# Block products summed in place in PSUM, and merge gates set between the recurrences

## The chip, the cores and the metric

The kernel runs on one core of one Trainium2 chip. The metric is the device time of one execution in microseconds (us). Before the change three runs gave 2738.37, 2735.38 and 2736.16 us, median 2736.16 us.

A core has five engines that matter here, each with its own instruction queue, worked off in order: TensorE (PE: matmuls, and PEld: the loading of their stationary operand), VectorE (DVE), ScalarE (ACT), GpSimd (POOL), and SyncE (SP, which here issues the DMAs). They wait for each other through semaphores. Matmul results land in PSUM, which has 8 banks of 128 partitions x 512 float32; PE writes it, DVE and ACT read it.

## The reference, cut to what matters

One layer of a hybrid mixer over 2048 tokens of width 1024, in float32:

```
h = rmsnorm(x, norm_g);  u = h @ w_in            # one wide input projection
A: RG-LRU   (lru_x, lru_z): conv of 4 taps, two block-diagonal gates, a linear scan, times silu(lru_z)
B: mLSTM    (m_x, m_o, m_z): conv of 4 taps, silu, chunkwise matrix memory
C: HGRN2    (h_q, h_f, h_i, h_z);  D: GLA (g_q, g_k, g_v, g_lr, g_z): gated linear attention in chunks
merged = sum over the 4 branches of sigmoid(merge_n) * (y_n @ w_branch[n])
out = rmsnorm(x + merged @ w_out, final_g)
```

The projection makes, among others, 32 channel tiles (128 channels each) of merge gates and 4 + 4 tiles for the RG-LRU.

## The kernel before

The tokens go in two halves of 1024 (called A and B here; A runs from about 52 us on, B from about 1422 us on). For each half there is a stretch of *pairs* (`ahead_pairs`), then the mixers B, C and D (`mixers`), then the branch projections and gates (`merge`) and the output projection (`outp`). In A and B alike the pairs take some 700 us, a quarter of the time each.

**A pair** (`ip_pair`) is the projection of two tiles of 128 channels for 1024 tokens. It is a 2 x 2 block product (channels tile 0 or 1, tokens 0 to 511 or 512 to 1023, contraction halves of 512 channels) in Winograd's form: seven block products in place of eight. The products are named by their left operand, a block of the input or a sum of blocks: `a11`, `a12`, `a22`, `s1`, `s2`, `s3`, `s4`. The input blocks and their sums are made once per half (`split_blocks`, lines L306 and L375 to L378). The weight blocks b11, b12, b21, b22 of each pair come by DMA; their sums are made on DVE (`wsum`, L427: four per pair). Each product splits its weight block into a high and a low float32r part, high by ACT (L416, tile `wh`), low by POOL (L417, tile `wl`), six buffers of each, and then issues 12 matmuls (L422): 4 contraction tiles x (high x high, high x low, low x high).

Each of the seven products has a PSUM bank of its own, handed out round and round over all 8 banks (`bank8`; the banks' tiles are called `pb` and `mx`). The first is copied out by ACT (`c11`, L437). The outputs c11, c12, c21, c22 are tiles in SBUF (`arena`), and the sums of products are formed there by DVE: seven additions per pair, each of one SBUF tile and one bank (`add`, L431).

When a pair is done its `fin` runs: for an RG-LRU pair (`r`, four per half) silu, a convolution (L704, L706), two gates of 12 matmuls in all (L735) with their tanh, exp and sqrt (L744) on ACT, and a scan on DVE (L748); for the paths (`z`) a silu (L477) or, for the two pairs of `m_x`, a convolution with its silu on DVE and ACT (L704, L706, L763; `mconv`); for merge gates (`g`, 13 pairs per half) a tanh or nothing, and a DMA to DRAM; for `d` the decays of HGRN2. The outputs live in 10 arena units, room for two and a half pairs.

**What sets the order.** `GORD` is a list by hand of which pairs are written in which order: `r`, `z`, `g`, `d` with a count; `t` switches the activation table, `m` runs a piece of mLSTM's rows. Beyond that a list scheduler with a cost model orders each engine's queue: instructions have priorities (`prio`: EV for evacuations and weights, LAT for the RG-LRU's and the convolution's tail, which comes later), and the order it finds is fixed in the program. On the chip each engine then works its queue in that order, waiting where a semaphore isn't there yet.

Of the kernel before, what the change touches and what calls it, by code (L numbers as in the profile page):

```python
# [17 lines left out]
HT = 1024  # tokens of a half  # L18
DM = 1024
KT = 8  # k tiles of d_model  # L20
U = 516  # columns of one arena unit
NU = 16  # arena units that stay
NA = 4  # tiles of two units that are the arena's outside of the fast products
NY = 8  # the same, and branch outputs in the merge
NP = 6  # merge gates (of 32) computed between the mixers
NE = 5  # of these, so many for the first tokens while the others are split
EPS = 1e-6
NPB = 2  # PSUM banks of the input projection; the other ones are the mixers'
NG = 10  # arena units of the fast products; the other ones are what follows them
PRE = (("mx", 4), ("mo", 4), ("mz", 4), ("hq", 4), ("hz", 4), ("gz", 4), ("gq", 2), ("gk", 2))  # paths to DRAM, with their tiles  # L30
# [11 lines left out]
GORD = [('r',1),('z',2),('r',1),('z',2),('r',1),('z',2),('r',1),('z',6),('g',8),('t',0),('m',0),('g',1),('m',0),('g',1),('m',0),('g',1),('m',0),('d',0),('m',0),('g',99),('d',1),('z',2)]  # L42
NORM = {"hz": "hnw", "gz": "gnw"}  # gate paths with the norm's weight in them
SILU = ("lz", "mz", "hq", "hz", "gz")
FILL = [0, 2, 0, 0, 0, 1, 0, 0, 1, 0, 0, 0, 2, 0]  # merge gates projected before each stage of the mixers

# columns of the packed per-channel vectors
# [10 lines left out]
# channel-major column tiles of the input projection, in the order of wc  # L58
# [10 lines left out]
# constants that depend on shapes alone  # L69
# [29 lines left out]
class Arena:  # L99
    """Units of U columns, handed out in program order, round and round; pairs start at even units."""  # L100
# [47 lines left out]
class Trunk:  # L148
# [107 lines left out]
    def proj_ch(self, pieces, rh, rl, sink, ns=(0, 1)):  # L256
        """128 columns of a product for 512 tokens at a time from weight pieces of 4 k tiles
        each: sink(token slice, PSUM [128, 512])."""
# [23 lines left out]
    def ip_tok(self, pieces, ncol, evac, single=8):  # L282
        """Token-major column group: evac(first chunk, PSUM [128 tokens, chunks, ncol]); chunks one by one from some."""
# [10 lines left out]
    def ip_tok_k(self, pieces, evac, ks):  # L294
        """The same for 256 columns, k outermost: the operands' tiles are done with one by one."""
# [13 lines left out]
    def split_first(self, xs):  # L309
        """The normalised input of the first tokens"""  # L310
# [7 lines left out]
    def load_first(self, xs):  # L318
        """The first tokens, and merge gates from them before the norm's factor is known"""
# [40 lines left out]
    def split_blocks(self, xs, st):  # L360
        """The other blocks (two of tokens by two of channels) that the products take: one more as it
        is, four sums; the block left out goes to DRAM."""
# [22 lines left out]
    def restore_block(self):  # L385
        """The block left out of the products, where its sum was."""
# [13 lines left out]
    def ip_pair(self, t0, t1, fin):  # L400
        """Two column tiles of 1024 tokens each; fin of both, [128, 3 free + 1024]."""
# [9 lines left out]
        def product(x, w):  # L411
# [6 lines left out]
            ps = self.bank8()  # L418
            for k, (xh, xl) in enumerate(self.op[x]):
                ws = slice(k * 128, (k + 1) * 128)  # L420
                for i, (wp, xp) in enumerate(((hi, xh), (hi, xl), (lo, xh))):
                    nc.tensor.matmul(ps, wp[:, ws], xp, start=(k == 0 and i == 0), stop=(k == 3 and i == 2))  # L422
# [6 lines left out]
        def add(o, x, y):  # L429
            with self.prio(self.EV):  # L430
                V.tensor_tensor(o, x, y, op=ALU.add)  # L431
# [1006 lines left out]
def layout(i):  # L1438
    """The inputs laid out for the kernel: no arithmetic on the data."""
    f = {k: np.asarray(v) for k, v in i.items()}  # L1440
    z = {}
# [99 lines left out]
```

## Time and profile before

| | |
|---|---|
| median of 3 runs | 2736.16 us (2735.38 to 2738.37) |
| span of the profiled execution | 2737.5 us |
| PE busy | 2603.8 us (95%) |
| DVE, ACT, POOL busy | 1736.1, 1291.6, 1499.7 us |
| additions L431 | 462 (348 on `mx` banks and 114 on `pb` banks) |
| copies L437 | 66 |

The span of the profiled execution lies between the timed runs; no other time of it is shown. Times in the rows below are us from the span's start, durations ns where the view says so. PEclk is the share of TensorE's full clock that was granted: 1.00 is 2.4 GHz, and a stretch at 1.2 GHz counts half. "Idle before" is idle time of the engine ahead of an instruction and what ended it. A matmul's recorded duration is longer than the distance to the next one, since they overlap.

### The profile page before, as it was taken

The numbers are of one execution on the slowest core, as the hardware profiler recorded it, in microseconds if no ns is written. First come the engines' busy times: TensorE is split into PE (matmuls) and PEld (weight loads), VectorE is DVE, ScalarE is ACT, GpSimd is POOL, SyncE is SP. The second block draws the span as 40 slices with busy tenths as digits, with TensorE's granted clock in tenths as the row PEclk, the third lists the DMA queues.
The fourth block names the chain that finished last, engine by engine and source line by source line (L and its number), as shares of the span: only waits on it lengthen the run. The fifth ranks groups of instructions, "written<-read, shape, count | busy, mean of one in ns | idle before, by whom it ended". The sixth has DMA issues, their size and how long they took to land. (4 is left out here: it accounts for less than half of the span.)

```text
span 2737.5 us, 45829 instructions
## 1 busy us (share of the span) xinstructions
PE 2603.8 (95%) x16800; PEld 2153.6 (79%) x16800; DVE 1736.1 (63%) x2907; ACT 1291.6 (47%) x2763; POOL 1499.7 (55%) x1273
## 2 busy tenths in 40 slices
PE   7889999999989898999999999999999999999999
PEld 5667788877878876778977777888787888777789
DVE  8987853346667767743478878533477677776332
ACT  5554554334444565542465545533344445644433
POOL 5556644444546545567476666444455556554753
PEclk9999999999999999999999999999999999989999
DMA  6132334243454435795442322433335533458821
GB/s 227 61 109 89 101 119 139 98 145 103 148 170 128 121 121 189 253 317 165 155 138 94 110 91 89 139 116 108 135 113 179 167 118 106 146 190 308 273 93 74
DMA packets 227072, 393.03 MB, mean 144 GB/s; under 512 B 20720, under 2 KB 78080, under 8 KB 226848
## 3 DMA queue, kind: packets, MB, share of 16 engines
q1 hardware_dynamic: 226848, 390.11, 42.7%
q8 instruction: 132, 2.16, 0.3%
q14 instruction: 92, 0.75, 0.1%
HBM read 270.42 MB, written 119.60 MB: 142 GB/s over the span
## 5 line engine op out<-in xcount | busy, mean ns | idle before, releaser
L417 POOL TENSOR_TENSOR wl<-wr,wh 128x512 fp32r<-128x512 f32 x264 | 371.6, 1411 | 302.4 <-ACT wh L416 294.4
L417 POOL TENSOR_TENSOR wl<-gth,wh 128x512 fp32r<-128x512 f32 x198 | 284.4, 1437 | 294.6 <-ACT wh L416 284.2
L422 PE MATMUL mx<-s,wh 128*128 128x512 f32 x1296 | 408.5, 395 | 11.3 <-DVE s L306 4.7
L431 DVE TENSOR_TENSOR arena<-arena,mx 128x512 f32<-128x512 f32 x348 | 229.4, 681 | 221.8 <-PE mx L422 208.5
L250 POOL TENSOR_TENSOR wl<-wr,wh 128x512 fp32r<-128x512 f32 (+1 forms) x176 | 250.4, 1431 | 175.4 <-ACT wh L249 139.8
L422 PE MATMUL mx<-hh,wh 128*128 128x512 f32 x760 | 302.0, 397 | 11.9 <-DVE arena L431 10.2
L422 PE MATMUL mx<-hh,wl 128*128 128x512 f32 x760 | 302.3, 398 | 3.1 <-POOL wl L417 3.1
L422 PE MATMUL mx<-hl,wh 128*128 128x512 f32 x760 | 302.0, 397 | 2.0 <-DVE hl L306 2.0
L422 PEld LDWEIGHTS mx<-s,wh 128*128 128x128 f32 x1296 | 243.9, 188 | 70.6 <-DVE s L306 7.1
L268 PE MATMUL pb<-hh,wh 128*128 128x512 f32 x704 | 286.9, 409 | 7.4 <-ACT hh L1284 2.6
L268 PE MATMUL pb<-hl,wh 128*128 128x512 f32 x704 | 286.5, 407 | 5.8 <-DVE hl L1285 5.8
L268 PE MATMUL pb<-hh,wl 128*128 128x512 f32 x704 | 284.3, 404 | 0.0
L416 ACT ACTIVATE wh<-wr 128x512 fp32r<-128x512 f32 x264 | 164.5, 627 | 232.7 <-PE mx L422 98.4
L280 PE MATMUL pb<-wh,hh 128*128 128x256 f32 (+1 forms) x880 | 254.2, 290 | 3.7 <-ACT arena L1006 1.5
L422 PE MATMUL mx<-s,wl 128*128 128x512 f32 x648 | 256.2, 396 | 0.9 <-POOL wl L417 0.9
L280 PE MATMUL pb<-wl,hh 128*128 128x256 f32 (+1 forms) x880 | 253.4, 288 | 1.7 <-POOL wl L250 1.7
L280 PE MATMUL pb<-wh,hl 128*128 128x256 f32 (+1 forms) x880 | 253.5, 288 | 0.0
L416 ACT ACTIVATE wh<-gth 128x512 fp32r<-128x512 f32 x198 | 124.4, 629 | 246.6 <-DVE gth L427 201.6
L249 ACT ACTIVATE wh<-wr 128x512 fp32r<-128x512 f32 (+1 forms) x176 | 110.0, 629 | 161.9 <-PE pb L268 106.6
L422 PEld LDWEIGHTS mx<-hh,wh 128*128 128x128 f32 x760 | 144.3, 190 | 50.1 <-ACT arena L218 11.0
L422 PEld LDWEIGHTS mx<-hh,wl 128*128 128x128 f32 x760 | 143.6, 189 | 41.0 <-POOL wl L417 8.2
L422 PEld LDWEIGHTS mx<-hl,wh 128*128 128x128 f32 x760 | 144.0, 189 | 38.1 <-DVE hl L306 3.2
(614 smaller groups left out, 6177.6 us busy)
## 6 DMA issues: line engine op xcount, KB each, us to landing
wr<-in_wc_dram SPq DMA_DIRECT2D x246, 256.0 KB, 2.7
g<-arena SPq DMA_DIRECT2D x52, 512.0 KB, 3.4
gth<-in_wc_dram SPq DMA_DIRECT2D x66, 256.0 KB, 2.8
wr<-in_wb_dram SPq DMA_DIRECT2D x64, 256.0 KB, 3.0
hl<-y SPq DMA_DIRECT2D x32, 512.0 KB, 5.9
arena<-g SPq DMA_DIRECT2D x48, 256.0 KB, 3.9
arena<-in_xT_dram SPq DMA_DIRECT2D x32, 256.0 KB, 5.1
lw<-g SPq DMA_DIRECT2D x32, 256.0 KB, 3.4
```

Source lines behind the costliest of these rows:

```text
L249: nc.scalar.activation(hi, raw, AF.Copy)
L250: nc.gpsimd.tensor_tensor(lo, raw, hi, op=ALU.subtract)
L268: nc.tensor.matmul(ps, w[:, ws], h[:, ts], start=(k == 0 and i == 0), stop=(k == nk - 1 and i == 2))
L280: self.nc.tensor.matmul(v, h[:, cs], w[:, ws], start=(first and i == 0), stop=(last and i == 2))
L416: A.activation(hi, w, AF.Copy)
L417: G.tensor_tensor(lo, w, hi, op=ALU.subtract)
L422: nc.tensor.matmul(ps, wp[:, ws], xp, start=(k == 0 and i == 0), stop=(k == 3 and i == 2))
L431: V.tensor_tensor(o, x, y, op=ALU.add)
```

## The change

In `ip_pair` three banks (p, q, r) serve a pair instead of seven. A product with `first=True` starts a bank anew; the others are added by PE to what the bank holds, and the bank is read between two products: copied by ACT (four copies per pair, three more) or added by DVE (three additions per pair, four fewer). In `GORD` the first eight pairs of gates no longer follow the RG-LRU's and the paths' pairs in one block: two pairs come first of all, one each before the second, third and fourth RG-LRU pair, and three behind the paths. Numbers of matmuls, weight sums, splits and DMAs stay. Comments are gone from the file too.

```diff
-GORD = [('r',1),('z',2),('r',1),('z',2),('r',1),('z',2),('r',1),('z',6),('g',8),('t',0),...]
+GORD = [('g',2),('r',1),('z',2),('g',1),('r',1),('z',2),('g',1),('r',1),('z',2),('g',1),('r',1),('z',6),('g',3),('t',0),...]
...
-        def product(x, w):
+        def product(x, w, ps, first=False):
...
-            ps = self.bank8()
...
-                    nc.tensor.matmul(ps, wp[:, ws], xp, start=(k == 0 and i == 0), stop=(k == 3 and i == 2))
-            return ps
+                    nc.tensor.matmul(ps, wp[:, ws], xp, start=(first and k == 0 and i == 0), stop=(k == 3 and i == 2),
+                                     skip_group_check=not first)
...
-        def add(o, x, y):
+        def add(o, ps):
             with self.prio(self.EV):
-                V.tensor_tensor(o, x, y, op=ALU.add)
+                V.tensor_tensor(o, o, ps, op=ALU.add)
+
+        def copy(o, ps):
+            with self.prio(self.EV):
+                A.activation(o, ps, AF.Copy)
...
-        p = product("a11", b11)
-        with self.prio(self.EV):
-            A.activation(c11, p, AF.Copy)
+        p, q, r = self.bank8(), self.bank8(), self.bank8()
+        product("a11", b11, p, True)
+        copy(c11, p)
+        product("a12", b21, q, True)
+        add(c11, q)
         wsum(b11, b12, b11)
         wsum(w2, b22, b11)
-        p = product("s2", w2)
-        add(c21, c11, p)
-        p = product("s1", b11)
-        add(c12, c21, p)
+        product("s2", w2, p)
+        copy(c12, p)
+        product("s1", b11, r, True)
+        copy(c22, r)
         wsum(b12, b22, b12)
-        p = product("s4", b22)
-        q = product("s3", b12)
-        add(c22, c12, q)
-        add(c21, c21, q)
-        add(c12, c12, p)
-        p = product("a12", b21)
-        add(c11, c11, p)
+        product("s3", b12, p)
+        add(c22, p)
+        product("s4", b22, r)
+        add(c12, r)
         wsum(b21, b21, w2)
-        p = product("a22", b21)
-        add(c21, c21, p)
+        product("a22", b21, p)
+        copy(c21, p)
```

How instructions stand now, at three places. First PE in a stretch of gates of half A; `pb_98` is bank p of one pair and `mx_100` its bank r, `mx_102` is bank p of the next pair. Before, the products of a pair follow each other, each to the next bank:

```order
L422 MATMUL mx_99<-s_3_582,wl_93 128x512
L422 MATMUL mx_100<-s_4_583,wh_82 128x512 x2
...
L422 MATMUL mx_100<-s_7_586,wl_88 128x512
L422 MATMUL mx_101<-s_8_587,wh_83 128x512 x2
```

Now:

```order
L422 MATMUL pb_98<-s_3_582,wl_88 128x512
L422 MATMUL mx_100<-s_4_583,wh_83 128x512 x2
...
L422 MATMUL mx_100<-s_7_586,wl_89 128x512
L422 MATMUL mx_102<-hh_63,wh_87 128x512
...
L422 MATMUL mx_102<-hh_66,wl_93 128x512
L422 MATMUL pb_98<-hh_63,wh_84 128x512
...
L422 MATMUL pb_98<-hh_66,wl_90 128x512
L422 MATMUL mx_100<-s_8_587,wh_85 128x512 x2
```

Between `s2` (its end is the first row above) and `s3` into the same bank stand `s1` and the next pair's `a11`: two products, not one; between `s1` and `s4` into `mx_100` stand that `a11` and `s3`.

Second DVE where the convolutions of the two `m_x` pairs run in half A. L706 before and L709 now is a tap of the convolution, L763 and L766 its silu, L427 a weight sum, L431 an addition out of a bank. Before:

```order
L427 TENSOR_TENSOR gth_94<-gth_94,gth_95 128x512
L706 SCALAR_TENSOR_TENSOR arena<-arena,hmc 128x512 x6
L431 TENSOR_TENSOR arena<-arena,mx_100 128x512
L706 SCALAR_TENSOR_TENSOR arena<-arena,hmc 128x512 x2
L763 SCALAR_TENSOR_TENSOR arena<-arena 128x512
L431 TENSOR_TENSOR arena<-arena,mx_101 128x512
L763 SCALAR_TENSOR_TENSOR arena<-arena 128x512 x2
L706 SCALAR_TENSOR_TENSOR arena<-arena,hmc 128x512 x3
L431 TENSOR_TENSOR arena<-arena,mx_103 128x512 x2
```

Now:

```order
L431 TENSOR_TENSOR arena<-arena,pb_98 128x512
L709 SCALAR_TENSOR_TENSOR arena<-arena,hmc 128x512
L696 COPY carry<-arena 128x3
L709 SCALAR_TENSOR_TENSOR arena<-arena,hmc 128x512 x2
L431 TENSOR_TENSOR arena<-arena,mx_100 128x512
L695 COPY arena<-carry 128x3
L766 SCALAR_TENSOR_TENSOR arena<-arena 128x512
L709 SCALAR_TENSOR_TENSOR arena<-arena,hmc 128x512
L431 TENSOR_TENSOR arena<-arena,mx_102 128x512
L709 SCALAR_TENSOR_TENSOR arena<-arena,hmc 128x512 x3
L427 TENSOR_TENSOR wr_79<-wr_80,wr_79 128x512
```

The additions among the taps were those of the second RG-LRU pair; now they are those of the second `m_x` pair (`pb_98` and `mx_100`) and of the gate pair that stands ahead of that RG-LRU pair (`mx_102`). The row that held six taps in a run now holds three.

Third ACT behind the first RG-LRU pair: L744 before and L747 now is the sqrt of the RG-LRU, L437 and L435 a copy out of a bank, L416 and L417 the high part of a weight block, L707 the first tap of the `m_x` convolution. Before:

```order
L416 ACTIVATE wh_82<-wr_81 128x512
L744 ACT_TABLE_LOAD
L744 ACTIVATE arena<-arena 128x512
L416 ACTIVATE wh_84<-gth_94 128x512
L437 ACTIVATE arena<-mx_100 128x512
```

Now:

```order
L218 ACTIVATE arena<-arena,small 128x512
L747 ACT_TABLE_LOAD
L747 ACTIVATE arena<-arena 128x512
L417 ACTIVATE wh_87<-wr_79 128x512
L747 ACTIVATE arena<-arena 128x512
L707 ACTIVATE arena<-arena,hmc 128x512
L417 ACTIVATE wh_84<-wr_79 128x512
L435 ACTIVATE arena<-pb_97 128x512
L417 ACTIVATE wh_83<-gth_95 128x512
L435 ACTIVATE arena<-pb_98 128x512
```

The copy from `pb_97` is c22 = s1 of the first `m_x` pair; PE writes s4 to that bank only behind it. Over the program ACT has 47 table loads now, where there were 29: eight more in the pairs (two each behind the third and fourth RG-LRU pair of a half), ten more at the end of the mixers. The mixers' instructions are the same, but the scheduler has set them in another order in places.

## Rows read from the trace of the kernel before

**Rows 1.** The page: its span and PE's busy time.

```profile
span 2737.5 us, 45829 instructions
PE 2603.8 (95%) x16800; PEld 2153.6 (79%) x16800; DVE 1736.1 (63%) x2907; ACT 1291.6 (47%) x2763; POOL 1499.7 (55%) x1273
```

**Rows 2.** Windows: stretch, its length; busy (xinstructions) of PE, PEld, DVE, ACT, POOL; PEclk; DMA.

```profile
1700.00:1800.00 100.00, 100.00 (x433) 81.09 (x433) 52.39 (x77) 48.77 (x79) 50.96 (x38) 1.00 0.40 132
52.00:85.00 33.00, 23.49 (x91) 16.66 (x92) 33.00 (x49) 12.97 (x22) 22.25 (x15) 0.95 0.14 40
85.00:200.00 115.00, 101.28 (x401) 78.02 (x400) 103.63 (x132) 62.12 (x96) 66.63 (x45) 0.94 0.26 87
200.00:400.00 200.00, 199.17 (x857) 160.35 (x856) 144.09 (x178) 102.00 (x164) 122.80 (x87) 1.00 0.33 110
1422.00:1440.00 18.00, 14.55 (x60) 10.59 (x59) 13.25 (x11) 9.90 (x19) 18.00 (x13) 1.00 0.36 126
1440.00:1600.00 160.00, 146.76 (x609) 116.04 (x608) 131.71 (x165) 81.50 (x130) 92.94 (x66) 0.97 0.26 89
```

**Rows 3.** PE's waits from 85 to 200, then from 1440 to 1600: total, times, longest.

```profile
PE mx L422 <- DVE arena L431: 6.8, 2, 5.1
PE pb L422 <- POOL wl L417: 3.3, 3, 1.7
PE pb L422 <- ACT wh L416: 1.6, 1, 1.6
PE pb L735 <- POOL wl L725: 1.3, 2, 1.0
...
PE mx L422 <- DVE arena L431: 6.4, 2, 5.1
```

**Rows 4.** Windows around the longest waits of each half.

```profile
130.00:142.00 12.00, 8.74 (x25) 6.27 (x25) 12.00 (x14) 5.97 (x11) 7.49 (x5) 0.72 0.24 70
160.00:170.00 10.00, 5.53 (x17) 4.28 (x18) 9.93 (x15) 4.52 (x8) 2.23 (x3) 0.83 0.16 60
```

**Rows 5.** DVE from 84 to 178: the window, then groups by line (busy us, mean ns).

```profile
84.00:178.00 94.00, 81.06 (x313) 61.93 (x313) 88.54 (x116) 46.20 (x72) 48.66 (x33) 0.93 0.25 87
...
L706 DVE SCALAR_TENSOR_TENSOR arena<-arena,hmc 128x512 f32<-128x512 f32 x24 | 25.0, 1075 | 0.1
L431 DVE TENSOR_TENSOR arena<-arena,mx 128x512 f32<-128x512 f32 x24 | 15.8, 678 | 0.5 <-ACT arena L437 0.5
L706 DVE SCALAR_TENSOR_TENSOR arena<-arena,pvt 128x512 f32<-128x512 f32 x12 | 11.1, 959 | 0.1
L763 DVE SCALAR_TENSOR_TENSOR arena<-arena 128x512 f32<-128x512 f32 x8 | 6.4, 814 | 0.0
L427 DVE TENSOR_TENSOR wr<-wr,wr 128x512 f32<-128x512 f32 x8 | 5.7, 708 | 2.1 <-DMA wr<-in_wc_dram 2.1
L427 DVE TENSOR_TENSOR gth<-wr,wr 128x512 f32<-128x512 f32 x4 | 4.6, 1147 | 0.0
L431 DVE TENSOR_TENSOR arena<-arena,pb 128x512 f32<-128x512 f32 x6 | 4.0, 676 | 0.0
...
L306 DVE TENSOR_TENSOR s<-arena,s 128x512 fp32r<-128x512 f32 x2 | 2.5, 1235 | 0.0
L427 DVE TENSOR_TENSOR gth<-gth,gth 128x512 f32<-128x512 f32 x3 | 2.0, 679 | 0.0
```

**Rows 6.** DVE's timeline ahead of PE's longest wait, which ends at 164.47.

```profile
149.34 5.59 DVE L706 SCALAR_TENSOR_TENSOR arena<-arena,hmc 128x512 f32<-128x512 f32 x6
...
159.18 3.35 DVE L706 SCALAR_TENSOR_TENSOR arena<-arena,hmc 128x512 f32<-128x512 f32 x3
162.45 1.88 DVE L431 TENSOR_TENSOR arena<-arena,mx 128x512 f32<-128x512 f32 x3
```

**Rows 7.** ACT's timeline behind the first RG-LRU pair.

```profile
110.58 1.28 ACT L744 ACT_TABLE_LOAD   x1
111.88 0.64 ACT L744 ACTIVATE arena<-arena 128x512 f32<-128x512 f32 x1
112.41 0.62 ACT L416 ACTIVATE wh<-gth 128x512 fp32r<-128x512 f32 x1
112.93 0.58 ACT L437 ACTIVATE arena<-mx 128x512 f32<-128x512 f32 x1
```

**Rows 8.** One line each: additions and copies out of banks, ns min/median/max.

```profile
L431 DVE TENSOR_TENSOR arena<-arena,mx x348: 654/680/691, 85.2 to 2119.2; 128x512 f32<-128x512 f32 x174
L437 ACT ACTIVATE arena<-mx x52: 574/580/602, 98.2 to 2096.7; 128x512 f32<-128x512 f32 x52
```

**Rows 9.** Windows of the mixers, half A and half B.

```profile
760.00:1120.00 360.00, 324.32 (x3366) 284.48 (x3368) 257.26 (x589) 177.58 (x520) 188.95 (x200) 0.94 0.46 145
2100.00:2460.00 360.00, 331.36 (x3406) 292.45 (x3405) 265.83 (x597) 182.51 (x529) 198.99 (x210) 0.94 0.48 152
```

More of the change, by code (lines that the diff above doesn't have):

```diff
@@ L41 @@
 LAT = -600
-GORD = [('r',1),('z',2),('r',1),('z',2),('r',1),('z',2),('r',1),('z',6),('g',8),('t',0),('m',0),('g',1),('m',0),('g',1),('m',0),('g',1),('m',0),('d',0),('m',0),('g',99),('d',1),('z',2)]
+GORD = [('g',2),('r',1),('z',2),('g',1),('r',1),('z',2),('g',1),('r',1),('z',2),('g',1),('r',1),('z',6),('g',3),('t',0),('m',0),('g',1),('m',0),('g',1),('m',0),('g',1),('m',0),('d',0),('m',0),('g',99),('d',1),('z',2)]
 NORM = {"hz": "hnw", "gz": "gnw"}
```

## The prediction, as put on record before the run

> **What bounds the kernel now.** I read the page first: PE is busy 95% of the span [rows 1], so only PE's idle time and its slow clock can be won by an edit that leaves all matmuls in place. Then a table of windows, to see where that idle time lies. In an undisturbed stretch of pairs PE issues 433 matmuls in 100 us, 0.231 us each, and everything else hides behind it [rows 2]. That rate prices the other stretches. From 85 to 200 us there are 401 matmuls, 92.6 us of work in 115: 22.4 us lost. From 1440 to 1600 there are 609, 140.7 us of work in 160: 19.3 us lost. The starts of the pairs lose 33 - 91 x 0.231 = 12.0 us (52 to 85; ten of these matmuls are small, so a little more) and 18 - 60 x 0.231 = 4.1 us (1422 to 1440). Behind them, from 200 to 400, 857 matmuls leave 2.0 us lost [rows 2]. So what this edit can win lies in two places of about 20 us, behind the first RG-LRU pair of each half.
>
> Third, the waits of PE there: 6.8 us for DVE's additions L431, 5.1 of them in one wait, then POOL's and ACT's weight splits, L431 again leading in half B with 6.4 us [rows 3]. Fourth, the clock in small windows: PEclk 0.72 from 130 to 142 means 0.28 x 12 x 2 = 6.7 us at 1.2 GHz, 0.83 from 160 to 170 another 3.4 us [rows 4]. Such a drop stands at the long waits, so one of them costs 1.7 to 3.4 us beyond its own length.
>
> Why are the additions late? DVE is busy 88.5 of 94 us from 84 to 178 [rows 5]; ahead of the long wait its timeline has six convolution taps in 5.59 us, three more in 3.35 us, and only then the three additions that free banks [rows 6]. DVE is the bound of these two stretches, PE of all others.
>
> **The change part by part.**
>
> *Additions and copies.* 264 additions of a median 0.68 us leave DVE, 198 copies of 0.58 us come to ACT [rows 8]: 180 us less and 115 us more, over 66 pairs. Outside the two stretches both hide behind PE: 1.7 us more per pair on ACT, which is busy about half the time [rows 2].
>
> *DVE's load behind the first RG-LRU pair.* From 84 to 178, DVE's 88.5 us hold 19.8 of additions, 12.3 of weight sums (15, 0.82 each), 2.5 of input splits, and 5.5 of the second RG-LRU pair's taps (half of 11.1) [rows 5]. The remaining 48.4 us belong to three pairs, the RG-LRU pair and the two convolution pairs. With four weight sums (3.3 us) and seven additions (4.6 us) per pair, DVE had 48.4 + 3 x 7.9 = 72.1 us to do while PE needs 3 x 84 x 0.231 + 12 x 0.231 = 61.0 us. Now a gate pair stands behind them and there are three additions (2.0 us): 48.4 + 4 x 5.3 = 69.6 us against 80.4 us. From 118% the load falls to 87%. The overload goes, and with it most of 22.4 + 19.3 = 41.7 us.
>
> *What stays of it.* DVE's order is still mixed. From the second `m_x` pair's c22 to the gate pair's c22 it holds 12 taps, 4 silus, 4 weight sums, 3 additions and 3 copies: 12 x 1.075 + 4 x 0.81 + 4 x 0.82 + 3 x 0.68 + 1 = 22.5 us by the means of rows 5 (0.34 per copy is an estimate from the same view's sum). PE has 82 matmuls between the two products that wait for these reads (a22 of either pair), 18.9 us. So a22 of the gate pair waits some 3.5 us in each half. The RG-LRU's own wait for POOL stays, 1.3 us [rows 3], and one clock drop of 3.4 us with these costs 1.7. With a us or two for what I do not see, 8 us per half stay, 16 in all. Bounds: nothing stays (0), or all of it (41.7).
>
> *The start.* Two gate pairs now come first, but PE still cannot pass the splits of the input sums, and the order sets a12 of the second pair behind s4 of the first. By 85 us PE will have done about 11 matmuls fewer than before, 2.5 us behind, and flows freely afterwards. Half B, where the splits come earlier, I take as even; 4 us either way bounds both.
>
> *Waits on banks.* Every pair has five reads that a later product into the same bank must wait for. In the order of the gates' stretch two products, 2 x 12 x 0.231 = 5.5 us, lie between a product's end and the next into its bank. A copy takes 0.58 us, an addition 0.68 [rows 8]; behind one or two other instructions of their queue they still fit. So I expect no wait there, and the pairs from 400 on keep 433 matmuls per 100 us. Behind an RG-LRU pair it is tighter: the copy c22 = s1 stands behind a table load, two sqrts, a tap and two splits, 1.28 + 0.64 + 0.62 + 0.64 + 0.62 + 0.62 = 4.4 us [rows 7], a tap priced as a sqrt, and the second sqrt waits for DVE. I take 1.3 us for each of the six later RG-LRU pairs, 8 us in all; the bounds are 0 and, if each waits like the longest wait now [rows 3], 6 x 5.1 = 31 us.
>
> *Table loads.* 18 more, 1.28 us each [rows 7], 23 us of ACT. Ten stand at the end of the mixers, where ACT is busy 178 of 360 us [rows 9]; I take them as hidden. Without that cover they cost 13 us. The loads' next instruction starts 0.02 us behind each of them [rows 7]. The Trainium skill (ScalarE: Activation LUTs, What ACT_TABLE_LOAD costs) adds a drain of about 1.38 us to the 1.28 us of each switch; by it the 18 would take 48 us of ACT. The row shows no such gap, so 23 us stand.
>
> *The mixers* have another order but the same instructions. PE idles 36 us there in half A and 29 in half B [rows 9]. I take no difference; 8 us either way is the bound, a quarter of the idle time of a half.
>
> *Sum:* 2737.5 - 41.7 + 16 + 2.5 + 8 = 2722.3 us against the profiled execution's span, which lies 1.3 us above the median of the runs. So about **2721 us**.
>
> **The rivals.**
>
> *Full relief* (2697 us). If 87% of load lets DVE keep up everywhere and no RG-LRU pair waits: 2737.5 - 41.7 + 2.5 - 1.3 = 2697. For it: from 200 to 400, with DVE busy 72%, only 2.0 us are lost [rows 2]. Against it: the 22.5 us of DVE beside 18.9 us of PE.
>
> *The change does not do what it says* (2736 us): the long waits are not the load of DVE but the order of its queue, and the new order holds as many late reads; each late read is now felt by PE at once, where eight banks took it up before. The 41.7 us stay, in other places. For it: the taps in runs [rows 6].
>
> *Slower* (2748 us). PE waits for bank reads behind every later RG-LRU pair. Place: s4 behind the copy c22 = s1, which stands on ACT behind the RG-LRU's second sqrt. Price: a wait as long as the longest now, 5.1 us, at six pairs, 31 us where the sum has 8: 2722.3 + 23 = 2745; a clock drop of 3.4 us at each, 1.7 us [rows 4], makes it up to 2755; the middle, less 1.3 us, is 2749, and 2748 where one of the six escapes a drop. It decides once that chain runs more than 5.5 us (two products) late; from there each us late is a us of PE, and at (41.7 - 16 - 2.5) / 6 = 3.9 us each the gain is gone. For it: four table loads instead of two stand in the chain for four of these pairs. Against: in the new order PE has 36 matmuls, 8.3 us, beside the chain.
>
> The Trainium skill (Perfetto Trace Analysis, Matmuls) speaks against the edit: independent groups should rotate through PSUM banks so that a read overlaps the next group's matmuls. If PE waited out all five reads of 66 pairs, that would be 330 x 0.63 = 208 us by rows 8, some 2900 us. The order still rotates, two other banks between; I give this 1%.
>
> **How the numbers follow.** Forecast 47%, full relief 14%, no effect 17%, slower 22% (the skill's case within it). A measurement of this kernel tells about 0.2%, 5.5 us, from no change. Forecast and full relief are faster: 61%; no effect is within 5.5 us: 17%; slower 22%. The forecast's own range is 2709 to 2731. To hold the time 8 times in 10 the range takes in full relief at its lower end and the slower case at its upper: 2696 to 2748.
>
> **What would show it.** Right: the pairs of half A end about 10 us earlier; from the third pair to the sixth PE's lost time is under 10 us where it was 22; DVE has idle time between its taps; from 400 on there are 433 matmuls per 100 us as before; additions 198, copies 264. The waits that are left name DVE's additions at a22 of the first late gate pair. Wrong: PE waits for ACT's copies at each RG-LRU pair (slower case), or the long DVE waits come back a pair later (no effect), or the mixers' stretch differs by more than 8 us, which no row here could tell.

## Result and profile after

The changed kernel takes a median of 2768.65 us (2768.11 to 2782.36, 4 runs) against 2735.77 us before: a ratio of 1.0126, 95% interval 1.0103 to 1.0149. The forecast was 2721 us, so it was wrong in sign, and the time lies 21 us above its range. The profiled execution's span is 28.8 us longer than that in [rows 1].

The page, its first lines:

```profile
span 2766.3 us, 45464 instructions
...
PE 2612.2 (94%) x16800; PEld 2149.8 (78%) x16800; DVE 1610.0 (58%) x2643; ACT 1409.2 (51%) x2979; POOL 1506.6 (54%) x1273
```

DVE lost 126 us of work and ACT got 118. PE has the same 16800 matmuls and is idle or slow for 29 us more. Windows of the pairs say where; they have the columns of [rows 2] and answer to its rows:

```profile
54.00:85.00 31.00, 21.11 (x70) 16.67 (x71) 31.00 (x44) 15.73 (x25) 19.66 (x13) 0.72 0.13 43
85.00:200.00 115.00, 107.64 (x451) 85.08 (x451) 80.83 (x102) 61.46 (x101) 65.45 (x44) 0.99 0.31 103
200.00:400.00 200.00, 195.78 (x840) 156.70 (x839) 108.73 (x124) 112.06 (x186) 118.23 (x85) 1.00 0.29 96
400.00:700.00 300.00, 297.46 (x1271) 232.55 (x1270) 150.48 (x186) 156.72 (x263) 148.08 (x110) 1.00 0.36 120
1430.00:1440.00 10.00, 5.54 (x12) 3.70 (x13) 8.46 (x9) 6.55 (x13) 10.00 (x8) 0.68 0.36 122
1440.00:1600.00 160.00, 151.72 (x641) 120.63 (x640) 103.81 (x122) 86.38 (x142) 93.86 (x65) 0.99 0.30 99
1600.00:2100.00 500.00, 493.85 (x2111) 389.75 (x2110) 261.33 (x312) 268.88 (x449) 263.78 (x192) 1.00 0.34 113
```

Two of these windows of the kernel before, which [rows 2] do not hold:

```profile
400.00:700.00 300.00, 300.00 (x1288) 236.17 (x1287) 145.99 (x219) 120.72 (x198) 136.79 (x106) 1.00 0.36 122
1600.00:2100.00 500.00, 499.42 (x2146) 397.22 (x2145) 296.52 (x404) 229.17 (x373) 261.61 (x191) 1.00 0.36 121
```

At 0.231 us a matmul, the two stretches that the forecast looked at did get better: 451 matmuls in place of 401, and 641 in place of 609. The quiet ones got worse: 840 in place of 857, 1271 in place of 1288, 2111 in place of 2146. The waits of PE in half A's pairs (engine, line, what it waited for, total, times, longest) have changed hands; these are the longest:

```profile
PE pb L422 <- ACT arena L435: 6.5, 1, 6.5
PE mx L422 <- ACT wh L417: 5.4, 4, 3.2
PE pb L422 <- DVE gv L628: 3.9, 1, 3.9
PE mx L422 <- DVE arena L431: 3.4, 4, 1.4
PE mx L422 <- DVE mqk L619: 3.4, 1, 3.4
PE mx L738 <- POOL wl L728: 2.5, 4, 0.6
PE mx L422 <- ACT arena L435: 2.0, 1, 2.0
```

The first, third and fifth of these rows are waits of the start, up to 85 us; what lies behind the first of them is told under *Which pairs*. Behind the start the additions, 6.8 us in [rows 3] for the stretch from 85 to 200 alone, are down to 3.4 for the rest of half A's pairs, and ACT's weight splits (L417) and copies (L435) hold 5.4 and 2.0. How a split comes to be late shows ACT's timeline behind the first `m_x` pairs (start, us, engine, line), ahead of a PE wait of 3.25 us that ends at 171.98:

```profile
169.33 0.63 ACT L218 ACTIVATE arena<-arena 128x512 f32<-128x512 f32 x1 [2.01 <-DVE arena L709]
169.86 0.80 ACT L707 ACTIVATE arena<-arena,hmc 128x512 f32<-128x512 f32 x1
170.78 0.63 ACT L218 ACTIVATE arena<-arena 128x512 f32<-128x512 f32 x1
171.31 0.61 ACT L417 ACTIVATE wh<-gth 128x512 fp32r<-128x512 f32 x1
171.83 0.58 ACT L435 ACTIVATE arena<-pb 128x512 f32<-128x512 f32 x1
172.31 1.07 ACT L435 ACTIVATE arena<-mx 128x512 f32<-128x512 f32 x2
```

The tanh at 169.33 waits 2.01 us for a tap on DVE (L709), and the split and three copies that PE needs stand behind it in ACT's queue. DVE's lateness reaches PE by way of ACT now.

Behind the pairs, at the end of half A's mixers, the waits of PE from 1120 to 1200 were, before:

```profile
PE pb L268 <- DVE gth L1311: 0.3, 1, 0.3
PE mx L985 <- DVE arena L1008: 0.3, 1, 0.3
```

and are now:

```profile
PE pb L268 <- DVE gth L1314: 6.4, 1, 6.4
PE mx L1097 <- ACT arena L1093: 2.2, 1, 2.2
```

Ahead of the first, the chain that the profile follows back goes through a DMA (`y<-mb`, 7.5 us) and DVE's splits behind it (L1288), and through no table load. ACT's timeline ahead of the second:

```profile
1158.42 1.28 ACT L1304 ACT_TABLE_LOAD   x1
...
1165.88 1.28 ACT L227 ACT_TABLE_LOAD   x1
1167.18 0.30 ACT L227 ACTIVATE ssq<-ssq,small 128x4 f32<-128x4 f32 x1
1167.49 1.28 ACT L1045 ACT_TABLE_LOAD   x1
1168.79 0.63 ACT L1045 ACTIVATE arena<-arena 128x512 f32<-128x512 f32 x1
1169.43 1.28 ACT L227 ACT_TABLE_LOAD   x1
1170.73 0.30 ACT L227 ACTIVATE ssq<-ssq,small 128x4 f32<-128x4 f32 x1
...
1171.57 1.28 ACT L1087 ACT_TABLE_LOAD   x1
```

A tanh of the merge (L1304) now has its table loaded ahead of this work. From there on each ln (L227) and each exp (L1045, L1087) that follows the other loads a table: four loads in 7 us. Before, such a ln and exp (L1084 there) stood ahead of the tanh (L1301) and needed none:

```profile
1157.13 0.33 ACT L227 ACTIVATE ssq<-ssq,small 128x4 f32<-128x4 f32 x1
1157.32 0.24 ACT L1084 ACTIVATE ssq<-ssq 128x4 f32<-128x4 f32 x1
1157.58 1.28 ACT L1301 ACT_TABLE_LOAD   x1
```

### The profile page after: what moved, and what is told of

It is laid out like the page before. It is cut to its first block, busy times and chain, and to the rows that moved or that the text cites. A ratio compares the mean times of both kernels' runs of the same rounds, so it can differ in the third digit from the quotient of the medians.

```text
span 2766.3 us, 45464 instructions
## 1 busy us (share of the span) xinstructions
PE 2612.2 (94%) x16800; PEld 2149.8 (78%) x16800; DVE 1610.0 (58%) x2643; ACT 1409.2 (51%) x2979; POOL 1506.6 (54%) x1273
## 4 chain that ended last, share of the span: by engine, by line
PE 66%; DVE 12%; DMA 7%; ACT 6%; issue 5%; POOL 4%; SPq 1%; POOLq 0%; ACTq 0%; DVEq 0%
PE mx L422 27%; PE pb L268 13%; PE pb L422 9%; PE pb L280 7%; DVE arena L709 1%; DMA mb<-rdram 1%; PE mx L1074 1%; PE mx L1075 1%; PE mx L280 1%; PE mx L1031 1%; POOL wl L250 1%; DVE arena L683 1%; PE mx L988 1%; ACT arena L218 1%; DVE arena L751 1%
## 5 line engine op out<-in xcount | busy, mean ns | idle before, releaser
L418 POOL TENSOR_TENSOR wl<-gth,wh 128x512 fp32r<-128x512 f32 x198 | 297.2, 1508 | 224.4 <-ACT wh L417 203.0
L422 PE MATMUL mx<-hh,wh 128*128 128x512 f32 x808 | 322.1, 399 | 24.2 <-DVE arena L431 7.7
L422 PE MATMUL mx<-s,wh 128*128 128x512 f32 x1040 | 331.1, 396 | 8.3 <-POOL s L306 4.5
L422 PE MATMUL mx<-hl,wh 128*128 128x512 f32 x808 | 321.7, 398 | 0.0
L422 PE MATMUL mx<-hh,wl 128*128 128x512 f32 x808 | 318.3, 399 | 3.0 <-POOL wl L418 3.0
L417 ACT ACTIVATE wh<-wr 128x512 fp32r<-128x512 f32 x264 | 164.0, 627 | 226.8 <-PE mx L422 137.9
L422 PEld LDWEIGHTS mx<-s,wh 128*128 128x128 f32 x1040 | 195.4, 188 | 60.7 <-POOL s L306 5.8
L431 DVE TENSOR_TENSOR arena<-arena,mx 128x512 f32<-128x512 f32 x142 | 96.6, 683 | 213.2 <-PE mx L422 155.4
L417 ACT ACTIVATE wh<-gth 128x512 fp32r<-128x512 f32 x198 | 124.7, 630 | 181.6 <-DVE gth L427 117.8
L422 PE MATMUL mx<-s,wl 128*128 128x512 f32 x520 | 205.9, 396 | 0.0
L422 PEld LDWEIGHTS mx<-hh,wh 128*128 128x128 f32 x808 | 153.9, 190 | 66.1 <-DVE arena L431 14.5
L422 PEld LDWEIGHTS mx<-hh,wl 128*128 128x128 f32 x808 | 153.4, 190 | 42.1 <-POOL wl L418 4.8
```

The source lines that it names most:

```text
L417: A.activation(hi, w, AF.Copy)
L418: G.tensor_tensor(lo, w, hi, op=ALU.subtract)
L422: nc.tensor.matmul(ps, wp[:, ws], xp, start=(first and k == 0 and i == 0), stop=(k == 3 and i == 2), skip_group_check=not first)
L431: V.tensor_tensor(o, o, ps, op=ALU.add)
```

## Experiments

All were compared with the kernel before on the same chip (its medians there are 2733.4 to 2736.3 us). To see where each one wins or loses, the table takes the time of PE's n-th matmul in the profiled execution (there are 16800 in each kernel) and sums stages between fixed n. *Starts*: matmuls 0 to 300 and 8400 to 8700. *RG-LRU*: 300 to 1600 and 8700 to 10000. *Late pairs*: 1600 to 2800 and 10000 to 11200. *Entry*, the last pairs and first rows of the mixers: 2800 to 3200 and 11200 to 11600. *Mixers* with the merge's begin: 3200 to 7400 (A) and 11600 to 15800 (B). The median is of several runs, the stages are of one execution, in us.

| kernel | median | ratio (95%) | starts | RG-LRU | late | entry | mixers A | mixers B |
|---|---|---|---|---|---|---|---|---|
| before | 2735.8 | 1 | 166.6 | 639.3 | 560.2 | 152.8 | 454.7 | 453.0 |
| changed | 2768.7 | 1.0126 (1.0103 to 1.0149) | 168.7 | 637.4 | 565.0 | 158.0 | 462.8 | 463.1 |
| gord: list alone | 2719.2 | 0.9947 (0.9928 to 0.9967) | 159.0 | 628.3 | 560.4 | 153.1 | 454.4 | 455.3 |
| banks: form alone | 2771.6 | 1.0137 (1.0117 to 1.0158) | 174.9 | 646.6 | 565.0 | 155.7 | 455.3 | 461.8 |
| start_old | 2758.1 | 1.0083 (1.0071 to 1.0095) | 158.6 | 639.3 | 564.6 | 156.2 | 466.0 | 460.0 |
| mid_old | 2773.3 | 1.0135 (1.0121 to 1.0150) | 170.4 | 633.0 | 566.6 | 157.6 | 461.7 | 481.5 |
| late_old | 2730.7 | 0.9985 (0.9972 to 0.9998) | 169.2 | 634.3 | 560.2 | 154.5 | 444.4 | 453.2 |
| reads_end | 2749.7 | 1.0051 (1.0032 to 1.0070) | 168.3 | 631.6 | 560.8 | 155.8 | 460.3 | 455.9 |
| copies_dve | 2787.2 | 1.0178 (1.0157 to 1.0200) | 171.0 | 649.8 | 569.6 | 161.3 | 461.9 | 460.2 |
| last2_new | 2742.1 | 1.0021 (1.0004 to 1.0037) | 159.0 | 627.9 | 560.4 | 159.1 | 462.6 | 467.4 |
| last2_old | 2754.8 | 1.0063 (1.0045 to 1.0081) | 171.7 | 637.1 | 564.6 | 154.8 | 454.9 | 460.4 |
| late_start_old | 2725.5 | 0.9962 (0.9948 to 0.9976) | 159.6 | 635.3 | 560.2 | 155.5 | 440.7 | 460.2 |
| after_tail | 2763.0 | 1.0109 (1.0087 to 1.0130) | 168.7 | 637.1 | 564.6 | 155.5 | 463.5 | 463.4 |
| before_tail | 2740.0 | 1.0018 (1.0001 to 1.0035) | 165.6 | 640.0 | 560.2 | 151.2 | 449.5 | 460.4 |
| last2_old_tail | 2746.8 | 1.0048 (1.0029 to 1.0066) | 173.1 | 635.8 | 564.6 | 154.6 | 448.8 | 457.0 |
| start_last_old_tail | 2734.4 | 1.0001 (0.9988 to 1.0014) | 158.3 | 638.4 | 564.6 | 155.0 | 458.6 | 453.2 |
| gord_tail | 2716.3 | 0.9921 (0.9893 to 0.9950) | 158.6 | 627.3 | 560.5 | 153.8 | 446.9 | 456.2 |

A profiled execution can lie off its kernel's median: those of `gord`, `mid_old` and `last2_new` took 2729.3, 2783.5 and 2755.3 us, 10 to 13 us more than the medians. The table leaves out matmuls 7400 to 8400, the end of half A. They take 148.7 to 152.1 us in most kernels, but 157.1 to 159.3 in `gord`, `reads_end`, `last2_new` and `late_start_old`, so that the columns of these four add up to some 6 us too little against the others.

**The list or the banks.** `gord` is the kernel before with the new `GORD`; `banks` is the changed kernel with the old one.

> The kernel before with the new list of pairs alone: seven banks and seven additions per pair, one copy. Theory 1 (the three banks of a pair cost the time, the list of pairs does not): the first two stretches behind an RG-LRU pair are relieved by the gate pairs between, eight banks take up late reads, nothing waits for a copy; 10 to 25 us faster than before, 2711 to 2726 us. Theory 2 (the list costs it: the two gate pairs at the start and the pairs set apart from each other): about as after, 2755 to 2770 us. Theory 3 (the list scheduler lays the mixers in another order whatever is changed ahead of them, and that order is what differs): the pairs differ little, the mixers by up to 16 us either way, as from before to after.

> The changed kernel with the old list of pairs: three banks, three additions and four copies per pair, all gate pairs behind the RG-LRU's and the paths'. Theory 1 (banks cost the time, the list of pairs gives back): no gate pair stands between the RG-LRU pairs and the paths, so PE waits more for reads there; as slow as after or slower, 2768 to 2790 us. Theory 2 (the list costs it): as before or faster, 2725 to 2740 us, since DVE has four additions less per pair. Theory 3 (the order of the mixers): the pairs as before within 5 us, the rest of the difference between the end of the pairs and the end of the half.

Measured 2719.2 and 2771.6 us: theory 1 both times. The list alone gives 16 us, in the starts and behind the RG-LRU pairs. The three-bank form costs 36 us with the old list and 49 with the new. Windows of `gord`:

```profile
85.00:200.00 115.00, 108.92 (x454) 86.01 (x454) 93.10 (x121) 53.35 (x86) 65.80 (x44) 0.98 0.30 105
...
400.00:700.00 300.00, 300.00 (x1287) 235.93 (x1286) 173.80 (x247) 131.78 (x215) 147.96 (x111) 1.00 0.37 126
1440.00:1600.00 160.00, 153.12 (x642) 122.19 (x641) 126.67 (x158) 80.28 (x127) 96.33 (x64) 0.98 0.29 100
1600.00:2100.00 500.00, 498.68 (x2145) 396.31 (x2144) 309.50 (x417) 231.48 (x379) 266.09 (x198) 1.00 0.37 123
```

With seven additions a pair, DVE is at 93 of 115 us and PE issues 454 matmuls, as many as with three (451). With the new list, the gate pairs between give the relief, and the fewer additions add nothing to it; behind it 1287 and 2145 matmuls stand as before. With the old list the fewer additions do relieve DVE, but ACT takes its place. PE's waits in `banks` from 85 to 200:

```profile
PE mx L422 <- ACT wh L417: 4.1, 1, 4.1
...
PE mx L422 <- ACT arena L435: 2.8, 1, 2.8
...
PE mx L422 <- DVE arena L431: 0.5, 1, 0.5
```

The wait of 5.1 us for additions [rows 3] is gone there, and 423 matmuls stand where there were 401; but from 1440 to 1600 there are 604 for 609, and the RG-LRU stage as a whole is 7.3 us longer.

**Which pairs.** The changed kernel with the old form (`ip_pair7`, seven banks) in some pairs; `start_old` has `np_ < 2`, `mid_old` `2 <= np_ < 15`, `late_old` `np_ >= 15`:

```diff
-                self.ip_pair(*tiles, fin)
+                (self.ip_pair7 if np_ < 2 else self.ip_pair)(*tiles, fin)
+                np_ += 1
```

> The changed kernel with the first two pairs of each half in the old form (seven banks, seven additions). Theory 1 (a bank that sums products fixes their order: before, PE began with whichever of s1, s3, s4, a22 had its input sums first, now s2 must come before s3 and a22 while s2's sums are formed late): the first 200 matmuls of the pairs take 4 to 5 us less in half A and 5 to 7 us less in half B, 10 us in all, 2755 to 2761 us. Rival (PE waits for reads of banks wherever it is): two of 33 pairs tell little, 2765 to 2770 us.

> The changed kernel with the old form in pairs 3 to 15 of each half, from the first RG-LRU pair to the last. Theory 1 (reads between products stand behind the recurrences' work in ACT's and DVE's queues): the stretch loses 5 us less in half A and 2 to 5 us less in half B, 2757 to 2763 us. Rival (the stretch costs nothing, DVE has fewer additions in it): 2768 us or slower.

> The changed kernel with the old form in pairs 16 to 33 of each half, behind the last RG-LRU pair. Theory 1 (the late pairs lose 2 and 5 us, and PE enters the mixers behind reads of banks, which also gives the mixers the order that they have in the changed kernel): 8 us in the pairs and up to 10 in the mixers, 2750 to 2760 us, and the order of the mixers is that of before. Rival (the loss of the mixers is chance of one execution, and the late pairs hide all): 2765 to 2770 us.

`start_old` took 2758.1 us, 10.5 less than the changed kernel, 10.1 of it in the starts: theory 1. The first 20 us of half B's pairs, in the changed kernel (its first matmul at 1429.9) and in `start_old` (at 1427.2):

```profile
1430.00:1450.00 20.00, 14.26 (x48) 10.31 (x49) 12.68 (x12) 11.10 (x20) 18.70 (x14) 0.83 0.27 88
```

```profile
1427.00:1447.00 20.00, 17.97 (x75) 13.35 (x74) 12.13 (x11) 9.37 (x19) 19.37 (x14) 1.00 0.29 103
```

48 matmuls against 75, 6.2 us of work. PE's idle time differs by 3.7 us (20 less the busy time); the rest is the slow clock, 0.83 granted against 1.00. What PE waited for there in the changed kernel is `s`, the sums of the input:

```profile
PE mx L422 <- POOL s L306: 4.5, 2, 3.2
```

With a bank for each product, the scheduler puts first whichever product has its operands first (before, half A ran a11, a12, s1, s3, a22, then s2 and s4; half B began with s3). In bank p the order a11, s2, s3, a22 is fixed, since each adds to what the last one left. In half A the wait of 6.5 us, which ends at 78.19, is put down to the copy of a11 out of bank p, but the input sums are as late there: in `reads_end` below, where no product waits for that copy, PE waits 4.7 us for a split of the sums (L305) in its place.

`mid_old` gained 4.4 us where the old form stands (RG-LRU), half of what theory 1 said, but its time did not fall and lies in the rival's range: mixers B took 18 us more, in an execution that was itself 10 us above the median. `late_old` missed its forecast by 20 us on the good side: 38 us less than the changed kernel, of which only 4.8 lie in the late pairs and 3.5 in the entry; 28 are in the mixers, which the edit does not touch.

**Reads between products, and on which engine.** In `reads_end` the copies and additions stay, and stand behind the last product of their bank. Each then reads the whole sum of its bank where the kernel needs a part of it, so the work is the same and the values are not the kernel's:

```diff
         product("a11", b11, p, True)
-        copy(c11, p)
...
         product("s2", w2, p)
-        copy(c12, p)
         product("s1", b11, r, True)
-        copy(c22, r)
         wsum(b12, b22, b12)
         product("s3", b12, p)
-        add(c22, p)
         product("s4", b22, r)
+        copy(c22, r)
         add(c12, r)
         wsum(b21, b21, w2)
         product("a22", b21, p)
+        copy(c11, p)
+        copy(c12, p)
+        add(c22, p)
         copy(c21, p)
```

> The changed kernel with the same products, additions and copies, but the copies and the addition out of bank p stand behind its last product and those out of bank r behind s4, so PE waits for no read between two products of a bank; it leaves out the values between (c11, c12, c22 take later sums). Theory 1 (part is the order that a bank fixes, part the reads between): half of the loss against the list alone stays, 2740 to 2755 us. Rival A (all of it is the reads): 2719 to 2735 us. Rival B (all of it is the fixed order): 2765 to 2770 us.

2749.7 us, 19 less, theory 1. The starts are as slow as in the changed kernel (168.3), so their loss is the fixed order and not the reads; the pairs behind them win 10 us (5.8 and 4.2), and the mixers, which again have another order, 9.7. The 10 us agree with the trace of the changed kernel, where PE waits for copies and additions behind the starts for 5.4 us in half A and 5.7 in half B. Against the list alone `reads_end` still loses 3.7 us in these two stages (3.3 and 0.4).

```diff
-                A.activation(o, ps, AF.Copy)
+                (A.activation(o, ps, AF.Copy) if o is c11 else V.tensor_copy(o, ps))
```

> The changed kernel with the three added copies of a pair (c12, c22, c21) on DVE in place of ACT. Theory 1 (in the stretch of the recurrences the copies and splits stand in ACT's queue behind silus that wait for DVE; elsewhere order decides): PE's waits for ACT's splits and copies in the pairs (14 us in half A) fall by a half, waits for DVE rise by as much, 2760 to 2775 us. Rival (ACT's queue is the cost): 2740 to 2755 us. Rival (DVE's load is still the bound): 2785 us or more.

2787.2 us: the last rival. PE's waits in half A's pairs for reads on DVE:

```profile
PE mx L422 <- DVE arena L435: 6.1, 6, 2.3
...
PE mx L422 <- ACT wh L417: 2.9, 3, 1.2
PE pb L422 <- DVE arena L435: 2.5, 2, 2.2
```

Splits wait less (2.9 for 5.4), but reads on DVE wait more: ACT was the better place for the copies.

**The stage behind the pairs.** `last2_old` is the changed kernel with the old form in the last two pairs (`np_ >= 31`), `last2_new` has the new form in these alone (old where `np_ < 31`), `late_start_old` has it in pairs 3 to 15 alone.

> The changed kernel with the old form in the last two pairs of each half alone (gq, gk). The old form in all of the last 18 pairs gave back 38 us, of which only 5 stood within the pairs. Theory 1 (the form of the last pairs decides in which order the scheduler lays the mixers behind them, and that order and PE's entry into the mixers cost the rest): 20 to 35 us faster than the changed kernel, 2734 to 2749 us, from the end of the pairs to the end of each half. Rival (reads of banks in all late pairs): 1 to 5 us, 2764 to 2768 us.

> The old form everywhere but in the last two pairs of each half, with the new list of pairs. Theory 1: the pairs as with the list alone, the mixers and their entry in another order and 20 to 35 us slower: 2739 to 2754 us. Rival: as the list alone, 2716 to 2724 us.

> The new list of pairs, and the new form in pairs 3 to 15 of each half alone, old in the first two and the last 18. If what the starts cost (10 us) and what the late pairs cost (38 us) add up: 2717 to 2724 us, about as the list alone. Rival (the effects overlap): 2726 to 2731 us.

`last2_new` is 23 us slower than the list alone, as theory 1 said, with starts, RG-LRU and late pairs equal to 0.4 us: two pairs of 33 move time in a stage whose code is the same. `last2_old` gave 14 us, between the two theories. `late_start_old` came out between its two cases.

What changes there is the order. The scheduler places the mixers by its simulated times, and these begin from the end of the last pair. Put together, entry and both mixers take 1052 to 1070 us in the nine kernels that end on an old pair (mean 1061) and 1072 to 1101 in the eight that end on a new one (mean 1083). Where PE's order in a half's mixers is the same but for a few small matmuls (2 to 17 of some 4200 places), the stage mostly is too: 453.0 and 455.3 in half B of `before` and `gord`; 614.6 and 614.7 us from matmul 3200 to 8400 of half A in the changed kernel and `start_old`. But `late_old` and `late_start_old`, alike as well, differ by 7 us in mixers B, so a single value says no more than that.

**The tables in the tail.** One dependency on ACT, without a wait, sets the merge's tanh behind the last exp (L1087):

```diff
-            A.activation(ss, ss, AF.Exp, scale=-0.5)
+            self.lastexp = A.activation(ss, ss, AF.Exp, scale=-0.5)
...
-                        A.activation(t[:, :512], t[:, :512], AF.Tanh, scale=0.5)
+                        self.after(A.activation(t[:, :512], t[:, :512], AF.Tanh, scale=0.5), self.lastexp)
```

> The changed kernel, and the tanh of the merge (L1304) set behind the last exp of the linear attention's norm (L1087) on ACT, so that no activation table is switched back and forth at the end of the mixers: 33 table loads in place of 47, 7 fewer in each half's tail. Theory 1 (the loads there stand on the path of PE: the 200 matmuls in which half A lost 18 us against before contain a chain of four of them): 10 to 20 us faster than after, 2749 to 2759 us. Rival (ACT idles half the time there and the loads are hidden; what differs is the order of the mixers): 2763 to 2771 us.

> The kernel before with the same edit at the end of the mixers: 25 table loads in place of 29, two fewer in each half's tail. Theory 1 (a table load there costs what it takes, 1.28 us each, when ACT's chain ends last): 0 to 5 us faster, 2731 to 2736 us. Rival (hidden): 2736 us. Theory 3 (each edit moves the scheduler's order of the mixers): up to 8 us either way.

> The changed kernel with the old form in the last two pairs, and the merge's tanh set behind the linear attention's last exp on ACT: no table is switched in the mixers' tail (before this edit six loads stand there in each half between the two). Theory 1 (the order of the tail costs: PE's waits for L1093's copies, 2.9 and 4.3 us in half A and 2.9 in half B, stand behind those loads, and the slow clock behind them takes 8.6 us more): 8 to 18 us faster than without it, 2737 to 2747 us. Rival (as where the same edit alone took 6 us off the changed kernel: waits move to the merge's DVE work): 2748 to 2753 us. Rival (hidden): 2755 us.

> The new list of pairs alone, with the same edit of the tail. Its half A has four table loads there, half B two, with waits of PE of 0.6 and 0.5 us. Theory 1: 0 to 5 us faster than the list alone, 2714 to 2719 us. Rival (the edit delays the merge's tanh and so its additions, as in the kernel before, where it gained nothing): 2719 to 2727 us.

> The changed kernel with the old form in the first two and in the last two pairs and with the edit of the tail. If the three causes are starts (10 us), the order behind the last pairs (14 us) and the loads in the tail (8 to 18 us), each by itself: 2727 to 2737 us, with the new form still in 29 of 33 pairs. Rival (bank reads in those 29 pairs cost what is left): 2740 to 2750 us.

`after_tail` came out 6 us lower, at the edge of the rival's range, where theory 1 had 10 to 20. Its mixers are no shorter in the table (463.5 and 463.4 for 462.8 and 463.1). PE's waits from 1110 to 1240, where no load stands ahead of them any more:

```profile
PE pb L268 <- DVE gth L1314: 6.4, 1, 6.4
PE mx L1097 <- ACT arena L1093: 3.4, 1, 3.4
```

The first is as before the edit; the second, 2.2 us with four loads ahead of it, is 3.4 without any. So in the changed kernel the loads are not shown to cost time. In `before_tail` nothing was won (2740.0). In `last2_old`, with six loads in each tail, the edit took 8.0 us off the median, at the edge of theory 1, and 9.5 off the mixers in the table. In both cases the intervals of the ratios with and without the edit overlap, so a gain of the edit is not shown to be clear of noise. (The old form's code stands ahead in these files: L1157, L1153 and L1374 are L1097, L1093 and L1314 of the changed kernel.) PE's waits in that stretch (matmuls 6600 to 7400) of `last2_old`, then of `last2_old_tail` from 1117 to 1238:

```profile
PE mx L1157 <- ACT arena L1153: 7.2, 2, 4.3
...
```

```profile
PE pb L268 <- DVE arena L1374: 3.1, 1, 3.1
...
```

The wait for ACT is gone here, and a part comes back as one for DVE; a third wait, 1.9 us for DVE, stays. `start_last_old_tail` adds up as theory 1 said: with the old form in four pairs and the edit of the tail, 34 of the 49 us are undone. `gord_tail` is the fastest, 2716.3 us; its interval overlaps that of the list alone, so the list is shown to gain, the tail's edit on top of it is not.

## Why the prediction was wrong

Three steps failed: the start was priced without the loss that a bank's fixed order brings, "I expect no wait there" was put down for the pairs from 400 on, and "I take no difference" for the mixers. And both parts of the edit were given a relief that the list brings alone: `gord` took 2719.2 us, close to the 2721 forecast for the two together.

The terms of the sum against the profiled execution, by windows of half A and half B. The pairs begin at 53.8 (1.8 us later) and end at 759.6 (3.9 later) in half A; in half B they begin at 1429.9 (7.5 later) and end at 2130.4 (18.2 later).

| term | predicted | measured |
|---|---|---|
| starts | +2.5 | +7.7 |
| the two stretches | -25.7 | -19.0 |
| later pairs | +8 | +25.9 |
| mixers and the rest | 0 | +14.2 |
| sum | -15.2 | +28.8 |

- *DVE's load* was read rightly: DVE is busy 80.8 of 115 us from 85 to 200 where it was 103.6 [rows 2], and the loss falls from 22.4 to 115 - 451 x 0.231 = 10.8 us, in half B from 19.3 to 160 - 641 x 0.231 = 11.9. The size is 6.7 us short. 3.5 us were kept for additions ahead of the gate pair's a22, which waits for none (the first `m_x` pair's a22 does, 1.3 us in either half); but the gate pair's a12 waits 3.2 us for a split on ACT, and its s3 for a copy on ACT, 2.0 us in half A and 1.2 in half B. Over the program DVE's busy time fell by 126 us where 180 were forecast; the additions took 162 with them, and other instructions of DVE took longer. What the step did not see is that the list does this alone (`gord`), so that the banks had nothing left to win.
- *The start* was counted as 11 matmuls behind. Half A lost 14.8 us from 54 to 85 where it was 12.0, and began 1.8 later: +4.6. Half B lost 10 - 12 x 0.231 = 7.2 us from 1430 to 1440 against 4.1 from 1422 to 1440: +3.1. In half A this is not idle time, which is 9.9 us (31 less the busy time) where it was 9.5. It is the clock: the 70 matmuls, 16.2 us of work, kept PE busy for 21.1 us, the 91 before, 21.0 us of work, for 23.5, as the granted clock was 0.72 and had been 0.95 [rows 2]. (The table's starts go on to matmul 300, at 100 us, and so hold a part of the list's relief.) The step weighed which products come first, but not that a bank that sums them takes away the choice, which `start_old` prices at 10 us.
- *Waits on banks* was the term mis-sized most within the pairs. "I expect no wait there, and the pairs from 400 on keep 433 matmuls per 100 us" fails: they have 1271 / 3 = 424. From 200 to 400 PE lost 4.0 us more, from 400 to 700 3.9; from 1600 to 2100 8.1. To the end of the pairs it is 3.0 in half A and 6.9 in half B, by what is left of 3.9 and 10.7. Six waits of 1.3 us were priced for, s4 behind the copy c22 = s1 at each later RG-LRU pair, and none of them is there. The two longer waits for ACT's copies behind the starts are the gate pair's (2.0 us, ending at 194.23, and 1.2, at 1562.05), ahead of the second RG-LRU pair's gates, and the product that waits is s3. Behind the six pairs PE waits for splits (0.8 us), for POOL's gate splits (0.6) and for work on DVE (0.4 to 1.2), and at the last pairs for additions (1.4 and 2.2). Reads of banks on both engines hold 5.4 and 5.7 us of the waits, and `reads_end` shows 10 us to be the reads themselves.
- *The mixers* were put at no difference, 8 us as the bound. From the end of the pairs to the next start or the end of the program it is 3.6 us more in half A and 10.6 in half B, and 18 in the mixers of the table; with it goes the order that the last pairs bring about (`last2_new`). The prediction had named a difference of more than 8 us there as a sign of being wrong. The step took a like number of instructions for a like time. That the bound was a quarter of the idle time of a half was a choice without a row; the sign could not have been told from one.
- *Table loads hidden* stays open: in the tail of the mixers PE waits 2.2 us for L1093 behind four loads, but in `after_tail`, without them, 3.4 us. The medians fall by 6 and 8 us where six or eight loads go in a half, within the noise, and not where two go (`before_tail`). The next instruction follows each load in 0.02 us here as in [rows 7].
- *The rivals*: slower at 2748 us had the right sign, and bank reads do cost time, but not at the place it named, and it had neither the starts nor the stage behind. The rule of the Trainium skill (Perfetto Trace Analysis, Matmuls: independent groups should rotate through banks, so that a read overlaps the next group's matmuls) had the right direction: the form costs 36 to 49 us here. The estimate of some 2900 us from it was far off, as most reads did overlap the two products between; `reads_end` puts the reads at 10 us in the pairs.

What stays open: 18 us between `start_last_old_tail` and `gord_tail`. By the table 15 are in the pairs (11 RG-LRU, 4 late), where reads and the fixed order were not told apart in that kernel; the rest is in the mixers. Nor was the mixers' order changed by itself, with the pairs untouched: that it costs the time is read from the two groups of kernels.

## What to carry to other kernels

Summing products in a PSUM bank saves additions, but it fixes their order, and PE waits for a read between two of them wherever the reading engine is late: look first at where operands arrive out of order and at what else stands in that engine's queue. When an edit has two parts, price each alone, since a relief that one gives cannot be won again by the other. And where a scheduler orders the program, an edit changes the stages behind it too: compare their orders, and allow for a loss there (18 us here in the mixers).

## What the runs showed of the hardware

Stretches that PE bounds repeat to a few tenths: the late pairs take 560.2 to 560.5 us in all seven kernels with the old form there. The mixers do not, with up to 7 us between two executions of the same order of PE, and whole runs of the kernel before spread from 2728.3 to 2745.9 us in one set of 18, where the three runs shown at first lay within 3. The 5.5 us called a measurement's resolution were too few for one run of each.

A wait in the mixers' tail costs clock as one in the pairs did [rows 4]: from 1120 to 1200 the granted clock (the number behind the engines) is 0.94 in the changed kernel and 1.00 before. Part of the slow time falls into the first wait itself. Behind the two waits the clock is 0.52 for 4.5 us and 0.57 for 4.0 us, which is 2.2 and 1.7 us beside the 8.6 of the waits.

```profile
1120.00:1200.00 80.00, 71.38 (x761) 55.37 (x760) 43.80 (x80) 38.48 (x84) 35.06 (x36) 0.94 0.79 272
```

```profile
1120.00:1200.00 80.00, 79.37 (x829) 61.24 (x830) 45.24 (x84) 41.66 (x120) 36.86 (x37) 1.00 0.89 306
```
